# State-space outputs beside the gate projections in a fused three-block kernel

## The chip, the cores and the metric

The kernel runs on one core of a Trainium2 chip. The metric is the device time of one execution in microseconds (us). The core has TensorE (PE in the profile; its weight loads are PEld), VectorE (DVE), ScalarE (ACT), GpSimd (POOL) and SyncE (SP), which issues the DMAs. Each engine works through its own queue in order.

## The reference

Three residual blocks run one after the other on a 1024 x 1024 activation: an attention block, a gated linear attention block and a state-space (S5) block. Only the last is touched:

```python
proj = h @ w_in
u, z = jnp.split(proj, [D_INNER], axis=-1)
...
bu = lax.complex(jnp.einsum('blgi,gpi->blgp', u32, jnp.real(b_bar)),
                 jnp.einsum('blgi,gpi->blgp', u32, jnp.imag(b_bar)))
...
_, states = lax.associative_scan(combine, (a, bu), axis=1)
y = (jnp.einsum('blgp,gip->blgi', jnp.real(states), c_re.astype(f32))
     - jnp.einsum('blgp,gip->blgi', jnp.imag(states), c_im.astype(f32)))
y = y + d_skip.astype(f32) * u32
y = jax.nn.gelu(y.reshape(bsz, seqlen, D_INNER))
y = y * jax.nn.sigmoid(y @ w_glu.astype(f32) + b_glu.astype(f32))
y = y * jax.nn.silu(z.astype(f32))
return y.astype(h.dtype) @ w_out
```

There are 128 groups of 16 channels; eight groups make an octet, so there are sixteen octets of 128 channels. The sequence is cut into 128 chunks of eight steps: within a chunk everything is a matrix product, and only the state at the chunk borders is scanned.

## The kernel before, in words

All products are made in float32r with a high and a low half, three matmuls for each (`mm3`, L190: L192 high x high, L193 high x low, L194 low x high). The weight stream `WStream` (L43) loads a piece of 128 x 1024 floats, casts its high half (L177, ACT) and subtracts the low half (L185, POOL or DVE) into a ring of six slots. Pieces are split in the order of `put`; a piece may be split as soon as fewer than six pieces ahead of it are unreleased (`pump`, L112), and a piece with a gate waits for that as well.

The S5 block (`s5`, L2125) has these stages:

- First stage (loop over `first`): the sixteen projections of u, then z's first three, and three steps behind them `states(o)`: chunk border inputs into `X` (128 states x 128 chunks x 128 groups, groups innermost) and the within-chunk part of y, which goes to DRAM (`yp_d`). After each fourth octet a scan over the borders is queued; its steps are DVE instructions on `X` (L2213 to L2265), issued a few at a time by `scan_on`.
- Gate stage (loop over `second`): the thirteen other projections of z, each 48 matmuls of 512 columns and a silu on ACT (L2154), with six scan steps behind each.
- Output stage (loop over `o`): for each octet the states' product (24 matmuls of 128 columns into a PSUM tile `big`, from `X` split into halves and the matrix `v_mat`), the sum with the stored part (L2361, DVE), gelu (L2366, ACT), and two octets later `y_out`: eight transposes (L2316), a cast (L2317) of the first half and a copy (L2319) of the second, and the low half (L2320). Beside it the first product of the GLU is begun (`glu_early`).
- GLU and output projection, in two halves of 512 columns: `gate` forms y times silu(z) beside the matmuls, then the sigmoid (L2467) and the halves of q (L2469, L185).

PSUM has four banks of 512 columns (`bank`) and two double banks (`big`). A scan holds two of the four banks; the staging pool `w4` has three tiles. `v_mat`'s low halves go to POOL for octets 0 to 3 and to DVE after that.

Of the kernel before, what the change touches and what calls it, by code (L numbers as in the profile page):

```python
# [21 lines left out]
S = 1024  # L22
# [2065 lines left out]
def s5_pieces(g):  # L2088

    A, ws = g.A, g.ws  # L2090
    w_in = A["s5_w_in_2"][0]
    q = Ctx()
    q.u_d = u_d = g.dram.tile([8, 16, P, P], F, name="su_d")
    q.spilled = spilled = [False] * S5_NO
    q.octet = octet = lambda o: slice(o * 8, o * 8 + 8)

    def put_u(o):
        return ws.put(8, P, [((slice(None),) * 3, u_d.rearrange("t i g c -> (t i) g c")[:, octet(o), :])],
                      gate=lambda: spilled[o], lo="dve")
# [12 lines left out]

    def put_cols(w, nk, c0, lo=None):
        return [ws.put(8, P, [((slice(None),) * 3, g.kview(w, k0 * P, 8, c0, P))], lo=lo) for k0 in range(0, nk, 8)]

    q.put_m, q.put_cols = put_m, put_cols
    q.first = []
    for i in range(S5_NO + S5_LAG):
        px = [put_u(i - S5_LAG), put_m(g.w_mat, i - S5_LAG, "pool"), put_T(i - S5_LAG)] if i >= S5_LAG else None
        q.first.append((i, px, put_cols(w_in, 8, i * P, "dve" if i == 1 else "pool")))  # L2120
    q.second = [(i, put_cols(w_in, 8, 2048 + i * P, "pool")) for i in range(S5_LAG, S5_NO)]
    return q


def s5(g, xn3, xstack, out):  # L2125
# [1 line left out]
    w_glu = A["s5_w_glu_2"][0]  # L2127
    w_out = A["s5_w_out_2"][0]
    NO, LAG = S5_NO, S5_LAG
    EARLY, GLU_AT, GLU_N = 1, (8, 14), 2  # L2130
    q = g.pieces.pop("s5") if "s5" in g.pieces else s5_pieces(g)
    u_d, spilled, octet, put_m, put_cols, first, second = (
        q.u_d, q.spilled, q.octet, q.put_m, q.put_cols, q.first, q.second)

    z_d = g.dram.tile([NO, P, S], F, name="sz_d")
    yp_d = g.dram.tile([NO, P, S], F, name="syp_d")
# [10 lines left out]
    def project(i, ids):  # L2147

        W = ws.take(ids)
        stage = stg.tile([P, S], F, name="w4")  # L2150
        for half in range(2):
            ps = g.bank()
            gemm_tr(g, hT, half, W, 0, P, ps, ids if half else None, True, later)
            nc.scalar.activation(half_of(stage, half, True), ps.rearrange("p (t c) -> p t c", t=8),  # L2154
                                 AF.Copy if i < NO else AF.Silu)
            ws.pump(1)
            if half == 0:
                yield
# [20 lines left out]
    third, pglu, pout = [], [[[] for _ in range(EARLY)], []], []  # L2179
    for o in range(NO):  # L2180
        if o in GLU_AT:
            for e in range(EARLY):
                pglu[0][e] += put_cols(w_glu[GLU_AT.index(o) * 1024:], 8, e * P)
        third.append([put_m(g.v_mat, o, "dve" if o > 3 else "pool"),
                      ws.put(8, P, X[:, :, octet(o)].rearrange("p n g -> p g n"), gate=lambda o=o: scanned[o // 4])])
# [4 lines left out]
    def states(o, ids):  # L2190

        U, W = ws.take(ids[:2])
        ps = g.big().rearrange("p (g n) -> p g n", g=8)
        for j in range(8):
            g.mm3(ps[:, j], [a[:, j, :] for a in W], [a[:, j, :] for a in U], True, True)
        nc.scalar.copy(X[:, 1:P, octet(o)], ps.rearrange("p g n -> p n g")[:, 0:P - 1])
        del ps
        yield
        T = ws.take(ids)[2]
        yp = stg.tile([P, 8, 8, 16], F, name="w4")  # L2200
        ps = g.big().rearrange("p (g n) -> p g n", g=8)
        for j in range(8):
            g.mm3(ps[:, j], [a[:, j, :] for a in U], [a[:, j, :] for a in T], True, True)
        nc.scalar.copy(yp.rearrange("c t g o -> c g t o"), ps.rearrange("c g (t o) -> c g t o", t=8))
        del ps
        ws.release(ids)
        nc.sync.dma_start(yp_d[o], yp.rearrange("c t g o -> c (t g o)"))
        ws.pump(2)

    G4, J = 32, 16  # L2210
# [66 lines left out]
    for i, px, pp in first:  # L2277
        gens = [states(i - LAG, px)] if px else []
        gens.append(project(i, pp) if i else begun)
        for _ in range(2):  # L2280
            for ge in gens:
                next(ge, None)
                scan_on(1)
        if px and (i - LAG) % 4 == 3:
            scans.append(((i - LAG) // 4, scan((i - LAG) // 4)))
    per = 6
    ws.hi_eng, ws.lo_eng = ["act"], ["pool"]
    early = []
    for i, ids in second:
        if i == NO - 1:  # L2290
            for o in range(2):
                early.append(stg.tile([P, 8, P], F, name="w4"))
                nc.sync.dma_start(early[o], yp_d[o].rearrange("c (t x) -> c t x", t=8))
        for _ in project(NO + i, ids):
            pass
        scan_on(per)
    assert not scans
    hold.clear()
    hp.close()

# [6 lines left out]
    ypend = deque()  # L2307

    def load_yp(o):
        nc.sync.dma_start(f32(y_hl[:, o]), yp_d[o].rearrange("c (a x) -> c a x", a=2))  # L2310

    def y_out():
        o, ya = ypend.popleft()
# [9 lines left out]
    accs, glu_w, glu_k = {}, {}, [0] * EARLY  # L2323

    def glu_step(half, e, k, ps):

# [7 lines left out]
    def glu_early(last, n):
        for e in range(EARLY):
            for _ in range(n):
                k = glu_k[e]
                if k > last:
                    break
                if k == 0:  # L2340
                    accs[e] = g.bank()
                glu_step(0, e, k, accs[e])
                glu_k[e] += 1

    AHEAD = 3
    ws.hi_eng, ws.lo_eng = ["act"], ["pool"]
    for o in range(2, AHEAD):
        load_yp(o)
    ws.pump(ws.RING)
    ws.age = 1  # L2350
    for o in range(NO):
        V, X_ = ws.take(third[o])
        ya = early[o] if o < 2 else stg.tile([P, 8, P], F, name="w4")
        if len(ypend) > 1:
            y_out()
        ps = g.big()
        for j in range(8):
            g.mm3(ps[:, j * P:(j + 1) * P], [b[:, j, :] for b in X_], [b[:, j, :] for b in V], True, True)
        part = ya.rearrange("c t x -> c (t x)") if o < 2 else f32(y_hl[:, o]).rearrange("c a x -> c (a x)")
        y4, part = [a.rearrange("c (t g o) -> c t g o", t=8, g=8) for a in (ya.rearrange("c t x -> c (t x)"), part)]  # L2360
        nc.vector.tensor_tensor(y4, part, ps.rearrange("c (g t o) -> c t g o", g=8, t=8), OP.add)  # L2361
        ws.release(third[o])
        ws.pump(3)
        if o >= GLU_AT[0] + 2:
            glu_early(o - 3, GLU_N)
        nc.scalar.activation(ya, ya, AF.Gelu_apprx_tanh)  # L2366
        ypend.append((o, ya))
        if o + AHEAD < NO:
            load_yp(o + AHEAD)
    glu_early(NO - 3, NO)  # L2370
    y_out()
    y_out()
# [197 lines left out]
```

## Time and profile before

| what | us |
|---|---|
| median of 3 runs (2654.11 to 2659.1) | 2658.63 |
| the profiled execution: its own time | 2654.64 |
| its span | 2652.9 |
| busy in the span: PE / PEld / DVE / ACT / POOL | 2440.0 / 1996.0 / 1675.6 / 1130.8 / 1024.5 |
| gate stage, to its last z matmul | to 2014.2 |
| output stage | 2014.2 to 2122.2 |

Times in the trace are us from the span's start. An engine's busy time says little by itself; what matters is which engine the others wait for in a stage. PE durations in the timeline overlap (they include the pipeline), so a matmul's cost is the distance from one start to the next.

### The profile page before, as it was taken

Reading aid. Unit: us, or ns where it says so; the run is one execution under the profiler, and the core shown is the slowest. Engines: PE = TensorE matmul, PEld = TensorE weight load, DVE = VectorE, ACT = ScalarE, POOL = GpSimd, SP = SyncE. Lnnn points to the kernel's source line nnn. Section 1 sums busy time; section 2 is a strip of 40 time slices with the busy share of each in tenths; the row PEclk is TensorE's granted clock in tenths of the full one; section 3 lists DMA queues with packets and bytes.
Section 4 is the critical chain, followed back from the end, with each engine's and each line's share of the span. In section 5 each row is a group of like instructions: output and inputs, shape, how many; then the busy total and the mean of one; then the engine's idle time right before and its main releaser. Section 6 shows DMA issues by size and latency. Waiting matters only on the chain.

```text
span 2652.9 us, 33078 instructions
## 1 busy us (share of the span) xinstructions
PE 2440.0 (92%) x11817; PEld 1996.0 (75%) x11817; DVE 1675.6 (63%) x2970; ACT 1130.8 (43%) x1907; POOL 1024.5 (39%) x780
## 2 busy tenths in 40 slices
PE   5887976999999999998988899999996999999998
PEld 4665654787777777777777778888885888888887
DVE  5888676777454666785777750376998855425632
ACT  5458895556432222325434334444223832223321
POOL 3515553322201566663444414444322632332321
PEclk8998987899999999999988999999997899999999
DMA  8312124221333554545333217777433753444441
GB/s 266 105 36 70 50 84 140 84 65 54 117 115 103 141 144 144 160 153 177 119 104 109 78 61 196 199 192 202 143 98 106 248 152 118 147 139 139 147 139 56
DMA packets 330173, 338.25 MB, mean 127 GB/s; under 512 B 67366, under 2 KB 248182, under 8 KB 329752
## 3 DMA queue, kind: packets, MB, share of 16 engines
q1 hardware_dynamic: 330008, 336.13, 41.3%
q8 instruction: 93, 1.52, 0.2%
q14 instruction: 72, 0.59, 0.1%
HBM read 239.19 MB, written 96.87 MB: 127 GB/s over the span
## 4 chain that ended last, share of the span: by engine, by line
PE 63%; DVE 16%; ACT 8%; issue 7%; POOL 2%; DMA 2%; SPq 1%; DVEq 0%; ACTq 0%; POOLq 0%
PE mm L192 16%; PE mm L194 16%; PE mm L193 16%; PE big L194 3%; PE big L193 3%; PE big L192 3%; ACT tku L828 2%; PE big L1160 1%; PE mm L1675 1%; DVE whl L185 1%; DVE xacc L1988 1%; PE mm L1259 1%; DVE rs_t L213 1%; ACT tka_d L837 1%; POOL rs_h L210 1%
## 5 line engine op out<-in xcount | busy, mean ns | idle before, releaser
L185 POOL TENSOR_TENSOR whl<-wraw,whl 128x1024 fp32r<-128x1024 f32 x158 | 386.5, 2454 | 862.8 <-ACT whl L177 777.1
L177 ACT CAST whl<-wraw 128x1024 fp32r<-128x1024 f32 (+1 forms) x279 | 287.9, 1048 | 396.0 <-PE mm L194 265.2
L185 DVE TENSOR_TENSOR whl<-wraw,whl 128x1024 fp32r<-128x1024 f32 (+2 forms) x121 | 181.7, 1510 | 295.7 <-ACT whl L177 295.5
L192 PE MATMUL mm<-h_hi,whl 128*128 128x512 f32 x768 | 306.2, 399 | 3.8 <-ACT uT L966 2.3
L192 PE MATMUL mm<-whl,h_hi 128*128 128x512 f32 (+1 forms) x720 | 290.0, 403 | 16.7 <-ACT whl L177 11.6
L194 PE MATMUL mm<-h_hi,whl 128*128 128x512 f32 x768 | 302.5, 394 | 0.0
L193 PE MATMUL mm<-h_lo,whl 128*128 128x512 f32 x768 | 302.5, 394 | 0.0
L193 PE MATMUL mm<-whl,h_hi 128*128 128x512 f32 (+1 forms) x720 | 283.4, 394 | 7.7 <-DVE whl L185 7.7
L194 PE MATMUL mm<-whl,h_lo 128*128 128x512 f32 (+1 forms) x720 | 283.2, 393 | 0.0
L193 PE MATMUL mm<-y_hl,whl 128*128 128x512 f32 x512 | 202.9, 396 | 0.5 <-DVE y_hl L2320 0.5
L192 PE MATMUL mm<-y_hl,whl 128*128 128x512 f32 x512 | 203.2, 397 | 0.0
L194 PE MATMUL mm<-y_hl,whl 128*128 128x512 f32 x512 | 202.8, 396 | 0.0
L192 PEld LDWEIGHTS mm<-h_hi,whl 128*128 128x128 f32 x768 | 144.9, 189 | 41.2 <-ACT uT L966 3.5
L192 PEld LDWEIGHTS mm<-whl,h_hi 128*128 128x128 f32 x720 | 138.6, 192 | 45.2 <-ACT whl L177 12.0
L194 PEld LDWEIGHTS mm<-h_hi,whl 128*128 128x128 f32 x768 | 144.7, 188 | 33.0
L193 PEld LDWEIGHTS mm<-h_lo,whl 128*128 128x128 f32 x768 | 144.9, 189 | 31.3 <-issue 0.2
L193 PEld LDWEIGHTS mm<-whl,h_hi 128*128 128x128 f32 x720 | 138.6, 192 | 34.4 <-DVE whl L185 9.1
L194 PEld LDWEIGHTS mm<-whl,h_lo 128*128 128x128 f32 x720 | 137.7, 191 | 29.0
L185 DVE TENSOR_TENSOR w<-w 128x512 f32<-128x512 f32 x48 | 71.4, 1513 | 105.8 <-DMA w<-sz_d 61.2
L193 PEld LDWEIGHTS mm<-y_hl,whl 128*128 128x128 f32 x512 | 96.5, 188 | 23.9 <-DVE y_hl L2320 0.9
L194 PEld LDWEIGHTS mm<-y_hl,whl 128*128 128x128 f32 x512 | 96.4, 188 | 23.4
L192 PEld LDWEIGHTS mm<-y_hl,whl 128*128 128x128 f32 x512 | 96.5, 188 | 22.9
(540 smaller groups left out, 5831.2 us busy)
## 6 DMA issues: line engine op xcount, KB each, us to landing
wraw<-in_s_w_glu_dram SPq DMA_DIRECT2D x64, 512.0 KB, 4.0
wraw<-in_gla_w_in_dram SPq DMA_DIRECT2D x40, 512.0 KB, 3.7
wraw<-in_s_w_in_dram SPq DMA_DIRECT2D x32, 512.0 KB, 4.2
wraw<-in_s_w_out_dram SPq DMA_DIRECT2D x32, 512.0 KB, 3.5
gv_d<-stg SPq DMA_DIRECT2D x32, 256.0 KB, 2.2
v_mat<-vc SPq DMA_DIRECT2D x32, 256.0 KB, 2.6
w_mat<-wo SPq DMA_DIRECT2D x32, 256.0 KB, 2.4
gz_d<-stg SPq DMA_DIRECT2D x32, 256.0 KB, 2.1
```

The source lines that it names most:

```text
L177: nc.scalar.copy(out, in_)
L185: e.tensor_tensor(out, a, b, op)
L192: nc.tensor.matmul(out, lhsT=lhs[0], rhs=rhs[0], start=start, stop=False)
L193: nc.tensor.matmul(out, lhsT=lhs[0], rhs=rhs[1], start=False, stop=False)
L194: nc.tensor.matmul(out, lhsT=lhs[1], rhs=rhs[0], start=False, stop=stop)
L210: nc.gpsimd.tensor_tensor(h, v, self.mhalf[:, :n], OP.pow)
L213: nc.vector.tensor_tensor(t, h, h, OP.mult)
L828: nc.scalar.activation(aj[:, :(b + 1) * P], keys[b], AF.Sign, bias=abias[:, q:q + 1], accum_out=asum[:, q:q + 1])
L837: nc.scalar.activation(asgn[:, c], asum[:, c], AF.Sign, bias=aneed[:, c])
L1160: nc.tensor.matmul(ps[:, c0:c1], lhsT=qt[:, j, :], rhs=kT[:, h // 4, e, c0:c1], start=(e == 0), stop=(e == 1))
L1259: nc.tensor.transpose(ps[:, o:o + P], sms[e][:, jj * P:(jj + 1) * P], g.ident)
L1675: nc.tensor.matmul(ps[0:16, i * P:(i + 1) * P], lhsT=B1[:, g0 + i, :], rhs=vc[:, i, 0:8, :].rearrange("p k o -> p (k o)"), start=True, sto ...
```

## The change

Twelve of the sixteen octets' output products move into the gate stage, one behind each of the first twelve z projections there. Their sum and gelu are written back into the octet's place in `X`, over its states, and the transposes read them there. Four octets stay in the output stage, where three `y_out` stand behind each product. z is stored as it comes; silu(z) is made in `gate` as z times sigmoid(z). The stored part of y keeps the matmul's layout. The scans get two steps instead of one in the second half of each step of the first stage, and four instead of six for each z projection.

```diff
-    q.second = [(i, put_cols(w_in, 8, 2048 + i * P, "pool")) for i in range(S5_LAG, S5_NO)]
+    q.put_z = lambda i: put_cols(w_in, 8, 2048 + i * P, "pool")
...
             nc.scalar.activation(half_of(stage, half, True), ps.rearrange("p (t c) -> p t c", t=8),
-                                 AF.Copy if i < NO else AF.Silu)
+                                 AF.Copy)
...
+    def put_out(o):
+        third.append([put_m(g.v_mat, o, "pool" if o < BESIDE else "dve"),
+                      ws.put(8, P, X[:, :, octet(o)].rearrange("p n g -> p g n"), gate=lambda: scanned[o // 4])])
+    for i in range(LAG, NO):
+        second.append((i, q.put_z(i)))
+        if i - LAG < BESIDE:
+            put_out(i - LAG)
...
-        nc.scalar.copy(yp.rearrange("c t g o -> c g t o"), ps.rearrange("c g (t o) -> c g t o", t=8))
+        nc.scalar.copy(yp.rearrange("c (g x) -> c g x", g=8), ps)
...
-                scan_on(1)
+                scan_on(1 + r)
...
+    def products(o):
+        V, X_ = ws.take(third[o])
+        ps = g.big()
+        for j in range(8):
+            g.mm3(ps[:, j * P:(j + 1) * P], [b[:, j, :] for b in X_], [b[:, j, :] for b in V], True, True)
+        ws.release(third[o])
+        ws.pump(2)
+        sums.append((o, ps))
+    def outputs():
+        o, ps = sums.popleft()
+        Xo = X[:, :, octet(o)]
+        gto = lambda a: a.rearrange("p (g t o) -> p g t o", g=8, t=8)
+        nc.vector.tensor_tensor(Xo.rearrange("p (g o) t -> p g t o", g=8), gto(parts.pop(o)), gto(ps), OP.add)
+        del ps
+        yield
+        nc.scalar.activation(Xo, Xo, AF.Gelu_apprx_tanh)
-    for i, ids in second:
...
-        for _ in project(NO + i, ids):
-            pass
-        scan_on(per)
+    for n, (i, ids) in enumerate(second):
+        ge, ou = project(NO + i, ids), outputs() if sums else iter(())
+        next(ge)
+        next(ou, None)
+        scan_on(2)
...
+        if n < BESIDE:
+            load_part(n)
+            products(n)
+        scan_on(2)
...
-            nc.tensor.transpose(pb[t // 4][:, t % 4 * P:(t % 4 + 1) * P], ya[:, t], g.ident)
+            nc.tensor.transpose(pb[t // 4][:, t % 4 * P:(t % 4 + 1) * P], X[:, :, o * 8 + t], g.ident)
         nc.scalar.copy(y_hi[:, o], pb[0])
         stage = wpool.tile([P, 512], F, name="w2")
-        nc.vector.tensor_copy(stage, pb[1])
+        g.copy("act" if o % 2 else "dve", stage, pb[1])
...
+    for o in range(BESIDE, NO):
+        if o + 1 < NO:
+            load_part(o + 1)
+        products(o)
+        ou = outputs()
+        for n in range(3):
+            y_out(done)
+            done += 1
+            next(ou, None)
+            ws.pump(1)
+            glu_early(2, done - 3)
...
         g.tt("dve" if e % 2 else "pool", t[:, 0], t[:, 0], t[:, 1], OP.mult)
+        nc.scalar.activation(t[:, 1], t[:, 1], AF.Sigmoid)
+        g.tt("pool" if e % 2 else "dve", t[:, 0], t[:, 0], t[:, 1], OP.mult)
```

First place: ACT's queue in the gate stage before, two z projections (`w` is the staging tile, with two evacuations for each).

```order
L2154 ACTIVATE w_17304<-mm 128x8x64
L177 CAST whl<-X 128x1024
L2154 ACTIVATE w_17304<-mm 128x8x64
L2154 ACTIVATE w_17393<-mm 128x8x64
L177 CAST whl<-wraw 128x1024
L2154 ACTIVATE w_17393<-mm 128x8x64
```

The same queue and stage in the changed kernel, one z projection and the start of the next:

```order
L2154 ACTIVATE w_16920<-mm 128x8x64
L177 CAST whl<-wraw 128x1024
L2154 ACTIVATE w_16920<-mm 128x8x64
L2318 ACTIVATE X<-X 128x128x8
L177 CAST whl<-wraw 128x1024
L177 CAST whl<-X 128x1024
L2154 ACTIVATE w_17052<-mm 128x8x64
```

A gelu (L2318) and the casts of `v_mat` and of an octet's states moved between the evacuations of two projections.

Second place: DVE's queue before, at the end of the last scan (L2262 is a scan's last instruction).

```order
L2262 TENSOR_TENSOR X<-X,mm 128x15x32
L2361 TENSOR_TENSOR w_17681<-w_17681,big_17751 128x1024
L2361 TENSOR_TENSOR w_17683<-w_17683,big_17785 128x1024
L185 TENSOR_TENSOR whl<-wraw,whl 128x1024
L2319 COPY w_17833<-mm 128x512
```

DVE's queue in the changed kernel, at the end of the last scan (there L2269):

```order
L2269 TENSOR_TENSOR X<-X,mm 128x15x32
L2315 TENSOR_TENSOR X<-w_17972,big_17974 128x8x8x16
L185 TENSOR_TENSOR whl<-wraw,whl 128x1024
L2315 TENSOR_TENSOR X<-w_18088,big_18090 128x8x8x16
L185 TENSOR_TENSOR whl<-wraw,whl 128x1024
L179 COPY w_18238<-mm 128x512
```

Before, the sums of all octets stood behind the whole scan, from octet 0 on; in the changed kernel only those of octets 10 to 15 (L2315) do, and those of 0 to 9 stand among the scan's steps.

Third place: PE's queue before, where the output stage's first transposes stand.

```order
L194 MATMUL big_17785<-whl 128x128
L2316 MATMUL mm<-ident,w_17681 128x128 x8
L192 MATMUL big_17837<-whl 128x128
L193 MATMUL big_17837<-whl 128x128
L194 MATMUL big_17837<-whl 128x128
```

PE's queue in the changed kernel at its first transposes, behind the product of octet 12:

```order
L194 MATMUL big_18196<-whl 128x128
L2348 MATMUL mm<-ident,X 128x128 x24
L192 MATMUL mm<-y_hl,whl 128x512
L193 MATMUL mm<-y_hl,whl 128x512
L194 MATMUL mm<-y_hl,whl 128x512
L192 MATMUL big_18282<-whl 128x128
```

ACT's queue in the changed kernel at the same place (L2349 evacuates the first half of an octet of y, L177 COPY the second of every other one):

```order
L177 CAST whl<-wraw 128x1024
L177 CAST whl<-X 128x1024
L2349 CAST y_hl<-mm 128x512 x2
L177 COPY w_18256<-mm 128x512
L2318 ACTIVATE X<-X 128x128x8
L2349 CAST y_hl<-mm 128x512
L177 CAST whl<-wraw 128x1024
L177 CAST whl<-X 128x1024
```

Eight transposes behind each product became twenty-four, read from `X`, and two split casts stand ahead of the first evacuations.

## Rows read from the trace of the kernel before

**Rows 1.** Busy time by stretch: each engine's us (instructions), granted PE clock, DMA share, GB/s.

```profile
1600.00:1870.00 270.00, 270.00 (x1563) 235.34 (x1562) 129.79 (x297) 116.48 (x133) 121.58 (x51) 1.00 0.71 195
1870.00:2014.00 144.00, 144.00 (x622) 116.89 (x621) 130.94 (x348) 29.39 (x39) 35.33 (x15) 1.00 0.36 113
2019.50:2043.50 24.00, 0.32 (x3) 0.18 (x3) 22.29 (x53) 3.09 (x4) 5.09 (x2) 0.54 0.08 25
2200.00:2250.00 50.00, 50.00 (x216) 40.23 (x215) 24.43 (x19) 14.87 (x18) 15.63 (x8) 1.00 0.40 119
```

**Rows 2.** Timeline of PE: end of the z projections, waits of the output stage.

```profile
2014.20 0.22 PE L192 MATMUL big<-whl 128*128 128x128 f32 x1
...
2043.35 1.97 PE L2316 MATMUL mm<-ident,w 128*128 128x128 f32 x8 [23.68 <-ACT w L2366]
...
2072.52 1.90 PE L2316 MATMUL mm<-ident,w 128*128 128x128 f32 x8 [1.71 <-ACT w L2366]
...
2122.22 0.49 PE L193 MATMUL mm<-y_hl,whl 128*128 128x512 f32 x1 [0.45 <-DVE y_hl L2320]
```

**Rows 3.** Chain that ended last (start, us), about the end of the scan.

```profile
2039.76 0.64 DVE mm L2261
2041.00 1.23 DVE w L2361
2042.24 1.06 ACT w L2366
```

**Rows 4.** Timeline of PE, one octet of the output stage at full clock.

```profile
2095.75 0.45 PE L192 MATMUL mm<-y_hl,whl 128*128 128x512 f32 x1
...
2097.19 1.04 PE L2316 MATMUL mm<-ident,w 128*128 128x128 f32 x8
2097.99 0.31 PE L192 MATMUL big<-whl 128*128 128x128 f32 x1
...
2100.70 0.44 PE L192 MATMUL mm<-y_hl,whl 128*128 128x512 f32 x1
```

**Rows 5.** Short stretches of the output stage, columns as in rows 1.

```profile
2072.00:2077.00 5.00, 4.48 (x26) 4.49 (x27) 4.97 (x5) 4.90 (x6) 2.46 (x2) 0.66 0.95 353
...
2087.00:2092.00 5.00, 5.00 (x19) 4.32 (x19) 4.12 (x4) 3.95 (x5) 1.55 (x2) 0.50 0.94 287
```

**Rows 6.** Groups of instructions, 2014 to 2122: busy us, mean ns, idle before.

```profile
L185 POOL TENSOR_TENSOR whl<-X,whl 128x1024 fp32r<-128x1024 f32 x14 | 41.2, 2942 | 57.0 <-ACT whl L177 52.1 <-DVE w L2361 3.5 <-DVE whl L185 1.5
L177 ACT CAST whl<-X 128x1024 fp32r<-128x1024 f32 x14 | 28.5, 2036 | 5.4 <-PE big L194 4.1 <-PE mm L194 1.3
L177 ACT CAST whl<-wraw 128x1024 fp32r<-128x1024 f32 x20 | 20.9, 1055 | 5.2 <-issue 3.2 <-ACT y_hl L2317 1.0 <-DMA wraw<-in_s_w_glu_dram 0.9
L2366 ACT ACTIVATE w<-w 128x1024 f32<-128x1024 f32 x16 | 17.0, 1062 | 24.5 <-DVE w L2361 24.4
L2361 DVE TENSOR_TENSOR w<-y_hl,big 128x1024 f32<-128x1024 f32 x14 | 16.9, 1210 | 3.3 <-PE big L194 3.3
L185 POOL TENSOR_TENSOR whl<-wraw,whl 128x1024 fp32r<-128x1024 f32 x6 | 14.3, 2408 | 0.0
L2320 DVE TENSOR_TENSOR y_hl<-mm,y_hl 128x512 fp32r<-128x512 f32 x16 | 10.9, 684 | 8.2 <-ACT y_hl L2317 8.2
L2317 ACT CAST y_hl<-mm 128x512 fp32r<-128x512 f32 x16 | 9.2, 574 | 1.2 <-PE mm L2316 1.2
```

**Rows 7.** Groups of instructions, gate stage (1870 to 2014).

```profile
L2239 DVE TENSOR_TENSOR mm<-X,mm 64x256 f32<-64x256 f32 x60 | 25.8, 430 | 2.1
L2262 DVE TENSOR_TENSOR X<-X,mm 128x480 f32<-128x480 f32 x28 | 18.3, 653 | 1.0
...
L2154 ACT ACTIVATE w<-mm 128x512 f32<-128x512 f32 x26 | 15.5, 595 | 53.4 <-issue 42.3 <-DMA sz_d<-w 7.8 <-PE mm L194 3.3
```

**Rows 8.** Instructions on the staging tile: count, ns least/median/most, first and last start.

```profile
L2467 ACT ACTIVATE w<-mm,cols x32: 667/684/691, 2130.6 to 2558.2; 128x512 f32<-128x512 f32 x32
...
L185 POOL TENSOR_TENSOR w<-w x16: 1289/1528/1754, 2129.3 to 2538.4; 128x512 f32<-128x512 f32 x16
```

More of the change, by code (lines that the diff above doesn't have):

```diff
@@ L2129, in s5 @@
     NO, LAG = S5_NO, S5_LAG
-    EARLY, GLU_AT, GLU_N = 1, (8, 14), 2
+    BESIDE = 12
     q = g.pieces.pop("s5") if "s5" in g.pieces else s5_pieces(g)
-    u_d, spilled, octet, put_m, put_cols, first, second = (
-        q.u_d, q.spilled, q.octet, q.put_m, q.put_cols, q.first, q.second)
+    u_d, spilled, octet, put_m, put_cols, first = (
+        q.u_d, q.spilled, q.octet, q.put_m, q.put_cols, q.first)
     z_d = g.dram.tile([NO, P, S], F, name="sz_d")
@@ L2178, in s5 @@
     nc.gpsimd.memset(X[:, 0], 0.0)
[L2179 to L2185, printed above, removed]
+    second, third, pglu, pout = [], [], [[[]], []], []
+    def put_out(o):
[6 more added lines that the diff above has]
+    for o in range(BESIDE, NO):
+        if o % 2 == 0:
+            pglu[0][0] += put_cols(w_glu[(o - BESIDE) * 512:], 8, 0)
+        put_out(o)
     for half in range(2):
@@ L2199, in states @@
         T = ws.take(ids)[2]
-        yp = stg.tile([P, 8, 8, 16], F, name="w4")
+        yp = stg.tile([P, S], F, name="w4")
         ps = g.big().rearrange("p (g n) -> p g n", g=8)
@@ L2203, in states @@
             g.mm3(ps[:, j], [a[:, j, :] for a in U], [a[:, j, :] for a in T], True, True)
-        nc.scalar.copy(yp.rearrange("c t g o -> c g t o"), ps.rearrange("c g (t o) -> c g t o", t=8))
+        nc.scalar.copy(yp.rearrange("c (g x) -> c g x", g=8), ps)
         del ps
         ws.release(ids)
-        nc.sync.dma_start(yp_d[o], yp.rearrange("c t g o -> c (t g o)"))
+        nc.sync.dma_start(yp_d[o], yp)
         ws.pump(2)
@@ L2279, in s5, with load_part @@
         gens.append(project(i, pp) if i else begun)
-        for _ in range(2):
+        for r in range(2):
             for ge in gens:
                 next(ge, None)
-                scan_on(1)
+                scan_on(1 + r)
         if px and (i - LAG) % 4 == 3:
             scans.append(((i - LAG) // 4, scan((i - LAG) // 4)))
-    per = 6
-    ws.hi_eng, ws.lo_eng = ["act"], ["pool"]
-    early = []
-    for i, ids in second:
[L2290 to L2293, printed above, removed]
-        for _ in project(NO + i, ids):
-            pass
-        scan_on(per)
-    assert not scans
+    parts, sums = {}, deque()
+    def load_part(o):
+        parts[o] = stg.tile([P, S], F, name="w4")
+        nc.sync.dma_start(parts[o], yp_d[o])
+    def products(o):
[14 more added lines that the diff above has]
+        nc.scalar.activation(Xo, Xo, AF.Gelu_apprx_tanh)
+    ws.hi_eng, ws.lo_eng = ["act"], ["pool"]
+    for n, (i, ids) in enumerate(second):
[3 more added lines that the diff above has]
+        scan_on(2)
+        for _ in ge:
+            pass
+        for _ in ou:
+            pass
+        if n < BESIDE:
+            load_part(n)
+            products(n)
+        scan_on(2)
+    assert not scans and not sums
     hold.clear()
@@ L2306, in s5, with y_out @@
     wpool = pool_of(g, xp, "s5w", bufs=2)
[L2307 to L2313, printed above, removed]
+    def y_out(o):
         pb = [g.bank(), g.bank()]
         for t in range(8):
-            nc.tensor.transpose(pb[t // 4][:, t % 4 * P:(t % 4 + 1) * P], ya[:, t], g.ident)
+            nc.tensor.transpose(pb[t // 4][:, t % 4 * P:(t % 4 + 1) * P], X[:, :, o * 8 + t], g.ident)
         nc.scalar.copy(y_hi[:, o], pb[0])
         stage = wpool.tile([P, 512], F, name="w2")
-        nc.vector.tensor_copy(stage, pb[1])
+        g.copy("act" if o % 2 else "dve", stage, pb[1])
         nc.vector.tensor_tensor(y_lo[:, o], pb[0], f32(y_hi[:, o]), OP.subtract)
         nc.sync.dma_start(y_d[o], stage)
-    accs, glu_w, glu_k = {}, {}, [0] * EARLY
+    accs, glu_w = {}, {}
+    glu_k = [0]
     def glu_step(half, e, k, ps):
@@ L2332, in glu_step, with glu_early @@
             ws.release(ids)
[L2334 to L2348, printed above, removed]
+    def glu_early(n, last):
+        while n and glu_k[0] <= last:
+            if glu_k[0] == 0:
+                accs[0] = g.bank()
+            glu_step(0, 0, glu_k[0], accs[0])
+            glu_k[0] += 1
+            n -= 1
     ws.pump(ws.RING)
     ws.age = 1
[L2351 to L2372, printed above, removed]
+    load_part(BESIDE)
+    done = 0
+    for o in range(BESIDE, NO):
+        if o + 1 < NO:
[8 more added lines that the diff above has]
+            glu_early(2, done - 3)
+    while done < NO:
+        y_out(done)
+        done += 1
+        ws.pump(1)
+        glu_early(2, done - 3)
     xp.close()
@@ L2453, in s5 @@
         for e in range(NO):
-            k0 = glu_k[e] if half == 0 and e < EARLY else 0
+            k0 = glu_k[0] if half == 0 and e == 0 else 0
             ps = accs.pop(e) if k0 else g.bank()
```

## The prediction

> **What bounds the kernel now.** I read the table of slices first, to find where TensorE is not busy late in the span, then busy times by stretch, then the timeline of TensorE there, then the chain. TensorE is busy without a break, at full clock, through the first S5 stage and the gate stage [rows 1], and again in the GLU. Between lies the output stage: 108.0 us from the first product behind the z matmuls, 2014.2, to the end of the last wait for an octet of y, 2122.2 [rows 2]. In 2019.5 to 2043.5 TensorE works 0.32 of 24 us while DVE works 22.29 [rows 1]: two products are through, and then transposes wait 23.68 us for gelu [rows 2], which waits for a sum that stands on DVE behind the last scan's steps [rows 3]. So here the scan ends last, not TensorE.
>
> What TensorE would need for the stage at full clock comes from one undisturbed octet [rows 4]: two GLU steps 2095.75 to 2097.19, 1.44 us (0.72 each); eight transposes to 2097.99, 0.80 us (0.10 each); 24 product matmuls to 2100.70, 2.71 us. Sixteen products 43.4, 128 transposes 12.8, fourteen GLU steps 10.1: 66.3 us. The other 41.7 of 108.0 are lost: 23.7 in the one wait, some 4 in short ones, the rest, 14, to the clock, which is at 0.50 to 0.66 in stretches after waits of a microsecond or two [rows 2, 5]. No change to this stage alone can bring more than 41.7 us.
>
> **The change, part by part.**
> Products into the gate stage. Twelve products of 2.71 us go behind z projections: 32.5 us. TensorE is without a break there, so nothing hides them; the gate stage ends at 2014.2 + 32.5 = 2046.7 if its feeders keep up. Per z projection TensorE then takes 11.1 (144 us for 13 [rows 1]) + 2.7 = 13.8 us. ACT's part: three split casts, two of 1.06 and one of 2.04, gelu 1.06 [rows 6], two evacuations of 0.60 [rows 7]: 6.4. POOL's: two low halves of 2.41 and one of 2.94 [rows 6]: 7.8. DVE's: four scan steps and a sum. Most steps are five instructions of some 0.43, 2.3 us with their gaps; in a scan's last stretch, seven steps, a step has two of 0.65 [rows 7], two nearly as long and five small ones, 3.6 us. That is 9 to 14.5 us a projection and 1.2 for the sum, over 13.8 only in a last stretch. All fit, and the ring lets a piece be split two octets ahead, 27 us. I take 0 for waits; from nothing to 1 us for each of twelve octets, 12 us, stays in the range. Below 0 it can't go, since TensorE had no gap there.
>
> More scan steps in the first stage. DVE works 129.8 of 270 us there [rows 1]; six steps instead of four for each 16.5 us (a projection of 11.1 and two states products of 2.7) make six times 2.3, 13.9 us, and 1.2 for u's low half. It still fits, and the low half of u, which shares DVE, is split more than one projection ahead. 0, and up to 3 if one end of a scan (3.6 us a step) delays it. What it buys: with six steps in each of the twelve rounds that have a scan, 72 instead of 48 are through before the gate stage, so 44 of 116 (29 for each scan) remain, 11 projections' worth at four. The scan is done before 2046.7, and the wait of 23.7 us has nothing left to wait for.
>
> The output stage that remains. TensorE: four products 10.8, 128 transposes 12.8, fourteen GLU steps 10.1: 33.7 us. What is late next is the evacuation. y_out needs two of three or four banks, and a bank comes free by ACT's cast (0.57) and DVE's low half (0.68), or by the copy of the same size [rows 6]. After each of the first two products ACT has a `v_mat` and an X split ahead of the casts, 1.06 + 2.04 = 3.1 us, which start only when the product has released its slots. First round: casts until +3.2, cast of y +3.8, low half +4.6, so the third octet's transposes start 3 us late; the next bank waits behind a sum of 1.21 on DVE: another 1.1. Second round, the same with one bank less: 3.1. Third and fourth round, two casts of w_glu in place of the X split: 1.2 each. The last four octets: DVE and ACT need 2.25 where TensorE needs 1.52: 2.9 in all. Together 12.5 us. From half of that, if TensorE's lead hides more, to 20.
>
> The transposes read X. Their data was one block; now each element lies 512 bytes behind the one before. No transpose of the trace does that. The nearest rows are the splits: ACT's cast takes 2036 ns from X against 1055 from a loaded piece, a factor of 1.93; POOL's 2942 against 2408, 1.22 [rows 6]. Bounds: nothing (0.10 each) up to ACT's 1.99 ns an element, 0.255 for 128, +19.8 us for 128 transposes. I take ACT's factor, 0.193: +11.9, of which the six octets of the two rounds that wait for ACT hide theirs: 7.4 us. DVE's write into X has the same stride and may double 1.21; it is off the path but for the one place above.
> [...]
>
> The clock. After waits of one or two microseconds it fell to 0.50 to 0.66 for some five us at a time while TensorE was 90% busy or more [rows 2, 5]. The first two rounds have such waits, but there ACT ends last, not TensorE. I take 2 us; from 0 to 10.
>
> silu taken apart. One more sigmoid on ACT, about the GLU's own 0.68, and one more product on DVE or POOL, at most POOL's 1.53 [rows 8], for each of 32 tiles. In the GLU ACT works 14.9, POOL 15.6 and DVE 24.4 of 50 us [rows 1], 11.1 us of TensorE's work for each tile, and nothing on TensorE waits for q before the output projection. 0; 2 us at most, for a late split.
>
> Sum: the output stage takes 33.7 + 12.5 + 7.4 + 2 = 55.6 and ends at 2046.7 + 55.6 = 2102.3, against 2122.2: 19.9 us less. Behind it all is as before. From the profiled execution's 2654.64 that makes 2634.7; the median of the runs is 4.0 above that execution, and from it I get 2638.7. I say 2637.
>
> **The rivals.**
> (a) No price on reading X and none by the clock: the stage takes 46.2, the gain is 29.3, the time 2625 to 2629. For it: a transpose's 0.10 us may have room for slower reads, and POOL lost only a factor of 1.22 [rows 6].
> [...]
> [...]
> (c) The gate stage isn't fed: TensorE waits for the X splits on ACT and POOL, 1 us an octet. That is +12, and the gain 8: 2647 to 2651. Against it: casts stand two octets ahead, and ACT and POOL have half of their time free.
> (d) Slower: the transposes from X take much longer than the splits show. The place is the weight load, 128 on TensorE's path in the output stage. The stage may take 2122.2 - 2046.7 = 75.5 us before nothing is gained; without transposes it has 10.8 + 10.1 + 12.5 + 2 = 35.4, so the point is 40.1 / 128 = 0.313 us a transpose, three times 0.10. At four times, 0.40, the stage is 86.6 and the kernel 11 us slower: 2666 to 2670. Against it: ACT's own rate would make 0.255.
>
> **How the numbers follow.** The forecast, 2631 to 2645, has 0.47; (a) 0.25; (b), or the upper bound of the X read with a slow clock, 0.11; (c) 0.09; (d) 0.08. A measurement of this kernel can tell about 0.2%, 5.3 us. Faster by more than that: the forecast, (a), (c) and a little of (b), 0.82. Same: most of (b), 0.10. Slower: (d), 0.08. The range runs from (a) with half of the evacuation's waits, a gain of 35 to 37 and so 2621, to (b) without gain, 2655; (d) and the tail beyond (a) are left out.
>
> **What would show it.** Right: TensorE without a gap and at clock 1.00 until about 2047; no wait over 5 us behind it; DVE's last scan step before 2030; the GLU's first full product at about 2102 instead of 2122. The transposes' distance of start to start tells (a), the forecast and (d) apart: 0.10, 0.19, over 0.31. Gaps ahead of L2348 released by ACT's cast or DVE's low half in the first two rounds show the evacuation. Wrong: waits of TensorE on L177 or L185 between z projections (c), a clock near 0.5 through the output stage (b), or a GLU that takes longer than before.

## The result and the profile after

The changed kernel takes 2673.2 us (median of four runs), the kernel before 2657.8 beside it: a ratio of 1.0062 (95% interval 1.0044 to 1.0079), 0.6% slower where 0.8% faster was forecast. One more run, the one profiled first, had a granted clock of 0.65 throughout, took 3524.9 us and is not used. The profile below is of an execution of 2671.92 us (span 2670.2), taken beside one of 2657.13 of the kernel before; lines of the kernel before are from the profile of span 2652.9. Ahead of this profile I had expected the loss in the output stage, with transposes 0.35 us or more apart and the z matmuls ending near 2047. Neither came; a third guess, a longer GLU, did.

Profiled executions differ by up to 8 us ahead of the S5 block, so I count from its first evacuation (L2154, first start in the row): 1578.0 before, 1578.5 after. Landmarks of the changed kernel, PE by line: last z matmul, first transposes, first full GLU step behind the last transposes, first matmul of the output projection. The instructions by tile, with first and last start:

```profile
L2154 ACT ACTIVATE w<-mm x64: 586/597/656, 1578.5 to 2062.0; 128x512 f32<-128x512 f32 x64
L194 PE MATMUL mm<-h_hi,whl x207: 390/393/404, 1880.2 to 2059.0; 128*128 128x512 f32 x104
L192 PE MATMUL big<-whl,q_hi x18: 388/389/395, 2287.4 to 2309.8; 128*128 128x512 f32 x18
```

The timeline of PE, start and duration:

```profile
2061.94 2.58 PE L2348 MATMUL mm<-ident,X 128*128 128x128 f32 x16
...
2117.89 0.48 PE L192 MATMUL mm<-y_hl,whl 128*128 128x512 f32 x1
```

The first and the last of the tile rows in the kernel before:

```profile
L2154 ACT ACTIVATE w<-mm x64: 582/597/602, 1578.0 to 2016.4; 128x512 f32<-128x512 f32 x64
L192 PE MATMUL big<-whl,q_hi x16: 388/390/393, 2290.8 to 2309.2; 128*128 128x512 f32 x16
```

The loss against the forecast falls into three pieces, counted in spans. The z matmuls end at 2059.0, 480.5 from the landmark, where 2046.7 was forecast (468.7): +11.8. The output stage takes 58.9 where 55.6 was forecast: +3.3. From the output projection's first matmul to the span's end it is 382.8, against 362.1 before: +20.7, where nothing was forecast. Together 35.8 of the 37.2 by which the span misses the forecast's 2633.0 (2652.9 less 19.9); the rest is 0.5 at the landmark and 0.9 in the first half of the GLU.

Busy time by stretch, columns as in rows 1, after:

```profile
1600.00:1850.00 250.00, 250.00 (x1451) 217.70 (x1450) 155.03 (x353) 104.01 (x120) 105.95 (x45) 1.00 0.72 189
1850.00:1870.00 20.00, 14.25 (x60) 11.18 (x59) 12.14 (x29) 6.05 (x7) 10.26 (x5) 0.74 0.55 170
1870.00:2050.00 180.00, 180.00 (x938) 152.52 (x938) 158.31 (x334) 75.18 (x74) 89.62 (x35) 1.00 0.50 157
2200.00:2250.00 50.00, 50.00 (x217) 40.54 (x216) 29.30 (x24) 17.45 (x23) 16.41 (x10) 1.00 0.36 106
2420.00:2470.00 50.00, 44.47 (x184) 35.46 (x183) 23.93 (x30) 15.23 (x25) 13.39 (x9) 0.93 0.46 137
```

The wait of 23.7 us of [rows 2] is gone and from 1870 to 2050 the gate stage runs without a gap, as forecast; then a matmul of its last z projection waits 2.76 us. But 5.75 us of TensorE's time are lost at the end of the first stage, with the clock at 0.74 there. And the GLU, which looks untroubled in the stretch that answers to the last of [rows 1], loses 5.5 us in 2420 to 2470. Waits of PE after, in time: in the first stage, in the last z projection for a bank that the scan uses (L2268 is a scan step), and in the GLU (timeline, idle time and releaser in brackets):

```profile
1855.13 0.33 PE L193 MATMUL big<-whl 128*128 128x128 f32 x1 [1.62 <-DVE whl L185]
1860.83 0.80 PE L192 MATMUL mm<-h_hi,whl 128*128 128x512 f32 x1 [2.92 <-ACT whl L177]
1863.26 0.80 PE L194 MATMUL mm<-h_hi,whl 128*128 128x512 f32 x1 [1.21 <-POOL whl L185]
2053.54 0.50 PE L192 MATMUL mm<-h_hi,whl 128*128 128x512 f32 x1 [2.76 <-DVE mm L2268]
2458.53 0.79 PE L192 MATMUL mm<-y_hl,whl 128*128 128x512 f32 x1 [5.53 <-ACT w L2492]
2572.14 0.79 PE L192 MATMUL mm<-whl,q_hi 128*128 128x512 f32 x1 [7.16 <-ACT w L2492]
2576.59 0.80 PE L192 MATMUL mm<-whl,q_hi 128*128 128x512 f32 x1 [2.80 <-ACT w L2492]
```

L2492 is the GLU's sigmoid, which empties the accumulator (L2467 before). What stands ahead of it, on ACT, and on SP (SPq: time in SP's queue, waiting included), after:

```profile
2457.28 0.63 ACT L2425 ACTIVATE w<-w 128x512 f32<-128x512 f32 x1 [12.99 <-DVE w L185]
...
2560.99 0.63 ACT L2425 ACTIVATE w<-w 128x512 f32<-128x512 f32 x1 [5.90 <-POOL w L185]
2561.53 0.67 ACT L2492 ACTIVATE w<-mm,cols 128x512 f32<-128x512 f32 x1
...
2563.51 1.99 ACT L177 CAST whl<-wraw 128x1024 fp32r<-128x1024 f32 x2
2570.88 0.63 ACT L2425 ACTIVATE w<-w 128x512 f32<-128x512 f32 x1 [5.38 <-DVE w L185]
```

```profile
2555.81 0.43 SPq L2419 DMA_DIRECT2D w<-sz_d  x1
2557.70 8.48 SPq L100 DMA_DIRECT2D wraw<-in_s_w_out_dram  x2
2566.22 0.43 SPq L2419 DMA_DIRECT2D w<-sz_d  x1
2568.05 8.57 SPq L100 DMA_DIRECT2D wraw<-in_s_w_out_dram  x2
```

This is a closed loop. The new sigmoid L2425, of the next tile, waits for z's product; that waits for z's load (L2419); SP issues this only when its two loads of weights have found raw slots (the stream's three tiles for loaded pieces that are not yet split), after 8.5 us; the slots come free by ACT's casts (L177) and the low halves made from them, and the casts stand behind L2425. So the GLU's own sigmoid, whose matmuls are done, waits some 5.5 us in every tile, and longer where stores of finished rows stand in SP's queue too (12.99 us ahead of 2457.28); there TensorE runs out of banks.

The slots' part of the loop isn't new. Waits of DVE's products and of ACT's cast of q in the GLU before (us in total, times, longest):

```profile
DVE w L185 <- DMA w<-sz_d: 61.2, 16, 7.0
ACT q_hi L2469 <- DVE w L185: 127.8, 31, 13.8
```

There too products waited for z's load, the cast of q stood behind them, and casts of weights behind that: in the longest of these waits SP's two loads found slots only after 8.54 us (from 2444.85); away from stores it took 4.2 to 4.7 us there, and 8.5 after. What did not stand behind those waits is the sigmoid that empties the accumulator (it waited for z's load once, 6.7 us), and TensorE has no wait behind 2125 in that trace.

### The profile page after: what moved, and what is told of

Its sections match the earlier page's. It is cut to its first block, busy times and chain, and to the rows that moved or that the text cites. A ratio compares the mean times of both kernels' runs of the same rounds, so it can differ in the third digit from the quotient of the medians.

```text
span 3523.1 us, 33099 instructions
## 1 busy us (share of the span) xinstructions
PE 3459.2 (98%) x11817; PEld 2308.1 (66%) x11817; DVE 1608.5 (46%) x2970; ACT 1157.9 (33%) x1946; POOL 1051.0 (30%) x804
## 4 chain that ended last, share of the span: by engine, by line
PE 93%; issue 2%; DVE 2%; ACT 1%; POOL 1%; DMA 0%; SPq 0%; DVEq 0%; POOLq 0%; ACTq 0%
PE mm L192 24%; PE mm L194 24%; PE mm L193 24%; PE big L194 4%; PE big L193 4%; PE big L192 4%; PE big L1160 2%; PE mm L1259 1%; PE mm L1675 1%; PE big L720 1%; PE mm L1227 1%; PE mm L1682 1%; PE mm L1225 1%; PE mm L1968 1%; PE mm L949 0%
## 5 line engine op out<-in xcount | busy, mean ns | idle before, releaser
L185 POOL TENSOR_TENSOR whl<-wraw,whl 128x1024 fp32r<-128x1024 f32 x167 | 412.6, 2477 | 1340.1 <-ACT whl L177 1079.8
L177 ACT CAST whl<-wraw 128x1024 fp32r<-128x1024 f32 (+1 forms) x279 | 286.8, 1046 | 560.2 <-PE mm L194 487.9
L192 PE MATMUL mm<-h_hi,whl 128*128 128x512 f32 x768 | 408.6, 532 | 0.0
L193 PE MATMUL mm<-h_lo,whl 128*128 128x512 f32 x768 | 403.9, 526 | 0.0
L194 PE MATMUL mm<-h_hi,whl 128*128 128x512 f32 x768 | 403.5, 525 | 0.0
L192 PE MATMUL mm<-whl,h_hi 128*128 128x512 f32 (+1 forms) x720 | 380.2, 528 | 0.0
L193 PE MATMUL mm<-whl,h_hi 128*128 128x512 f32 (+1 forms) x720 | 376.3, 523 | 0.8 <-DVE whl L185 0.8
L194 PE MATMUL mm<-whl,h_lo 128*128 128x512 f32 (+1 forms) x720 | 373.9, 519 | 0.0
L185 DVE TENSOR_TENSOR whl<-wraw,whl 128x1024 fp32r<-128x1024 f32 (+2 forms) x112 | 153.2, 1375 | 448.4 <-ACT whl L177 448.4
L192 PE MATMUL mm<-y_hl,whl 128*128 128x512 f32 x512 | 261.6, 511 | 0.0
L194 PE MATMUL mm<-y_hl,whl 128*128 128x512 f32 x512 | 260.1, 508 | 0.0
L193 PE MATMUL mm<-y_hl,whl 128*128 128x512 f32 x512 | 259.8, 507 | 0.0
L192 PEld LDWEIGHTS mm<-h_hi,whl 128*128 128x128 f32 x768 | 170.3, 222 | 94.9 <-issue 35.5
L194 PEld LDWEIGHTS mm<-h_hi,whl 128*128 128x128 f32 x768 | 167.2, 218 | 92.3 <-issue 34.9
L194 PEld LDWEIGHTS mm<-whl,h_lo 128*128 128x128 f32 x720 | 154.2, 214 | 87.4 <-issue 33.7
L193 PEld LDWEIGHTS mm<-whl,h_hi 128*128 128x128 f32 x720 | 153.0, 213 | 83.4 <-issue 34.7
L192 PEld LDWEIGHTS mm<-whl,h_hi 128*128 128x128 f32 x720 | 151.1, 210 | 83.5 <-issue 34.1
L194 PEld LDWEIGHTS mm<-y_hl,whl 128*128 128x128 f32 x512 | 106.1, 207 | 60.7 <-issue 20.0
L193 PEld LDWEIGHTS mm<-y_hl,whl 128*128 128x128 f32 x512 | 106.5, 208 | 59.2 <-issue 20.0
L192 PEld LDWEIGHTS mm<-y_hl,whl 128*128 128x128 f32 x512 | 106.3, 208 | 59.3 <-issue 20.1
```

The source lines that it names most:

```text
L177: nc.scalar.copy(out, in_)
L185: e.tensor_tensor(out, a, b, op)
L192: nc.tensor.matmul(out, lhsT=lhs[0], rhs=rhs[0], start=start, stop=False)
L193: nc.tensor.matmul(out, lhsT=lhs[0], rhs=rhs[1], start=False, stop=False)
L194: nc.tensor.matmul(out, lhsT=lhs[1], rhs=rhs[0], start=False, stop=stop)
```

## The experiments

Ten kernels, beside the execution above; each ratio is against the kernel before on the same chip. Kernels that ran on different chips are compared by these ratios, times 2657 us.

**The silu alone.** In the kernel before:

```diff
-AF.Copy if i < NO else AF.Silu)
+AF.Copy)
...
+        nc.scalar.activation(t[:, 1], t[:, 1], AF.Sigmoid)
+        g.tt("pool" if e % 2 else "dve", t[:, 0], t[:, 0], t[:, 1], OP.mult)
```

> The kernel before with one part of the change alone: gate's silu taken apart (projection copied, a sigmoid on ACT and a second product in the gated linear unit). Theory: the whole loss after 2119 us comes from this part, because the new sigmoid stands in ACT's queue ahead of the sigmoid that empties the accumulator of the tile before, and ahead of the casts that free the raw slots for which SP's queue waits before it issues the load of z: the stretch from the output projection's begin to the end, and the gated linear unit ahead of it, take 14 to 22 us more than in the kernel before, so about 2672 to 2680. Rival: the loss came from another part (the order of the products and of the loads, late output octets), and the sigmoid costs nothing, as the prediction had it: 2655 to 2660, and no wait of PE for w of the gated linear unit over 3 us.

Measured: 2685.3, ratio 1.0101 (1.0084 to 1.0118), 28 us slower; PE's waits for the GLU's sigmoid (L2469 here) 17.9 us in 4, and 387.3 us from the output projection's first matmul to the end, against 362.1. Above the theory's range, and far from the rival: this part alone turns the kernel before into a slower one.

**The silu undone** (the same lines of the changed kernel, the other way).

> The changed kernel with this one part undone: the gate projections are evacuated through Silu again, and the gated linear unit has one product per tile. Theory: the waits of 5.5, 7.2 and 2.8 us of PE for the sigmoid of the gated linear unit go, and the clock with them: 15 to 21 us less than the changed kernel, 2651 to 2658. On the other side stand two changes of ACT's function table per gate tile (Silu and Gelu in turns) in the gate stage, where ACT is under half busy: 0 to 5 us. Rival: the waits belong to the loads and stay: 2670 to 2676.

Measured: 2651.5, ratio 0.9977 (0.9967 to 0.9986), some 23 us less than the changed kernel. No wait of PE behind 2130 is left, and the rest from the output projection's first matmul takes 362.1 us again.

**The silu apart, but later in the queue.**

```diff
             g.sub("dve", q_lo[:, e], t[:, 0], f32(q_hi[:, e]))
+            if e + 1 < NO:
+                gate2(e + 1, zs[0])
```

`gate2` holds the sigmoid and the second product, taken out of `gate`.

> The changed kernel with silu still apart, but the new sigmoid and product of tile e+1 are written behind the sigmoid, product, cast and difference of tile e. Theory (the place in ACT's queue is what costs): the accumulator of tile e is emptied whatever the load of z does, the three waits go, 12 to 21 us less than the changed kernel: 2651 to 2660. Rival (the extra work on ACT, DVE and POOL is what costs, or the raw slots wait for the sigmoid all the same): 2666 to 2676.

Measured: 2651.9, ratio 0.998 (0.997 to 0.999), some 22 us less, with the same work as the changed kernel. The line of the stretch in which the changed kernel lost 5.5 us:

```profile
2420.00:2470.00 50.00, 50.00 (x216) 40.24 (x215) 28.94 (x38) 17.58 (x28) 17.14 (x12) 1.00 0.46 135
```

The rest takes 362.2 us. So the place in the in-order queue costs all of it, and the extra work nothing. ACT and SP in this kernel:

```profile
2460.56 0.63 ACT L2427 ACTIVATE w<-w 128x512 f32<-128x512 f32 x1 [1.99 <-POOL w L185]
2461.10 1.99 ACT L177 CAST whl<-wraw 128x1024 fp32r<-128x1024 f32 x2
...
2445.65 9.25 SPq L100 DMA_DIRECT2D wraw<-in_s_w_glu_dram  x2
```

The casts that free the slots still stand behind the new sigmoid (L2427 here), and SP still waits for slots, without cost to TensorE. What counts is that the sigmoid that empties the accumulator no longer stands behind the new one.

**u's low halves on POOL** in the first stage of the changed kernel.

```diff
-                      gate=lambda: spilled[o], lo="dve")
+                      gate=lambda: spilled[o], lo="pool")
```

> The changed kernel with one edit in the first stage: the low halves of u are made on POOL instead of DVE, so that no raw slot waits behind the doubled scan steps of DVE. Theory: PE's idle 5.7 us near 1855 to 1866 and the low clock behind them go, 8 to 12 us less than the changed kernel: 2660 to 2666. Rival 1: the first loads of the scan's tables stay late behind the raw loads, and the idle time moves to the gate stage: 2668 to 2676. Rival 2: POOL, which then has 12 differences of about 1.5 us per 50 us instead of 9, holds the slots instead: 2672 or more.

Measured: 2663.5, ratio 1.0024 (1.0012 to 1.0037), some 10 us less. The stretch that had 14.25 us at clock 0.74:

```profile
1850.00:1870.00 20.00, 20.00 (x119) 17.54 (x119) 16.65 (x40) 8.86 (x10) 9.51 (x4) 1.00 0.66 201
```

What had happened there, on DVE, SP and ACT of the changed kernel:

```profile
1853.29 0.65 DVE L2269 TENSOR_TENSOR X<-X,mm 128x480 f32<-128x480 f32 x1
1853.86 1.22 DVE L185 TENSOR_TENSOR whl<-wraw,whl 128x1024 fp32r<-128x1024 f32 x1
1862.08 0.23 DVE L2238 COPY mm<-scL 128x64 f32<-128x64 f32 x1 [7.00 <-DMA scL<-scan_d]
```

```profile
1841.20 6.25 SPq L100 DMA_DIRECT2D wraw<-kp_d  x8
1855.10 0.40 SPq L100 DMA_DIRECT2D wraw<-in_s_w_in_dram  x1
...
1856.17 0.54 SPq L2227 DMA_DIRECT2D scL<-scan_d  x1
```

```profile
1844.07 1.06 ACT L177 CAST whl<-wraw 128x1024 fp32r<-128x1024 f32 x1 [7.24 <-DMA wraw<-su_d]
...
1859.73 1.04 ACT L177 CAST whl<-wraw 128x1024 fp32r<-128x1024 f32 x1 [8.21 <-DMA wraw<-in_s_w_in_dram]
```

u's cast (its piece is loaded from su_d) was done at 1845.13, but its low half stood behind scan steps on DVE until 1855.08. Only then was its raw slot free, and SP issued the next load at 1855.10, the first since 1847.45; ACT's next cast waited 8.21 us for it, and PE behind that. From the S5 landmark to the last matmul of the projection ahead of the first product it is 292.0 us in the changed kernel (1870.54 less 1578.5) and 282.7 here (1865.04 less 1582.3): 9.3 us. To the last z matmul it is 480.5 and 473.0: the wait for the scan's bank is still there (2.7 us), and behind it matmuls of 512 columns lie 0.43 us apart from 2049.92 to 2052.90 here, while they lay 0.23 apart behind it in the changed kernel (2053.88 to 2058.99).

**Both edits.**

> Both edits in the changed kernel: the new sigmoid and product of tile e+1 behind those of tile e, and the low halves of u on POOL. Theory: the two causes are separate (one ends at 1870, the other begins after 2119), so their gains add: 22 us and 11 us less than the changed kernel, 2639 to 2646. Rival: one is hidden behind the other, or both are the clock's doing: 2649 to 2656.

Measured: 2643.5, ratio 0.9951 (0.9938 to 0.9965), some 29 us less than the changed kernel where the two gains make 32: within the noise the gains add, and the kernel is faster than before.

**The stored part loaded before the gate tile** instead of behind it, on top of both.

```diff
+        if n < BESIDE:
+            load_part(n)
         next(ge)
...
-            load_part(n)
             products(n)
```

> The kernel with both edits, and one more in the gate stage: the part of an octet is loaded before the gate tile whose products need it instead of behind it, so that DVE's sums no longer wait for it (18.7 us in 7 waits in the stretch after 1860 with u on POOL). Theory (the sums' waits push the last scan steps from about 2030 to 2049, and ACT's cast of octet 12 waits for these): the last product of octet 12 ends up to 9 us earlier, 4 to 9 us less than with both edits alone. Rival (DVE's own work in the gate stage sets the scan's end): within 2 us of it. A buffer of the same pool is held longer, which can cost on the other side: up to 3 us more.

Measured: 2635.3, ratio 0.9921 (0.9908 to 0.9935), 8 us less than with both: within the theory. DVE's last scan step, with both edits and with the third:

```profile
2048.57 0.65 DVE L2269 TENSOR_TENSOR X<-X,mm 128x480 f32<-128x480 f32 x1
```

```profile
2038.21 0.65 DVE L2269 TENSOR_TENSOR X<-X,mm 128x480 f32<-128x480 f32 x1
```

The z matmuls of this kernel, with their first and last start:

```profile
L194 PE MATMUL mm<-h_hi,whl x200: 390/392/404, 1880.2 to 2051.4; 128*128 128x512 f32 x100
```

The wait for the scan's bank is gone with it: 468.5 us from the landmark to the last z matmul, 473.0 with both edits. This is the fastest version measured, with the last one below.

**The sum in another order**, on top of both edits: `p g o t` in place of `p g t o` on either side, so that writes go in runs of 32 bytes and reads are strided.

> The kernel with both edits, and the sum walked in another order: the same elements, written in runs of 32 bytes and read with a stride from PSUM and from the part, instead of written with a stride of 512 bytes (1.99 us each). Theory (the stride of the writes sets the doubled duration): 1.2 to 1.4 us each, 16 sums, DVE 10 us freer in the gate stage and the end of the scan earlier by as much of it as lies in DVE's queue: 2 to 6 us less. Rival (the strided reads cost what the strided write did): 1.9 to 2.4 us each, within 2 us.

Measured: 2645.3, ratio 0.9963 (0.995 to 0.9975), no gain. The sums, in this kernel and in the one with both edits (least/median/most ns):

```profile
L2315 DVE TENSOR_TENSOR X<-w,big x16: 1890/1950/2153, 1898.2 to 2096.9; 128x1024 f32<-128x1024 f32 x16
```

```profile
L2315 DVE TENSOR_TENSOR X<-w,big x16: 1869/1992/2335, 1895.6 to 2097.2; 128x1024 f32<-128x1024 f32 x16
```

The durations are the rival's: with strided reads the sum takes as long as with strided writes. Whether it is the reads, or the writes in short runs, isn't separated.

**Transposing a matrix whose columns lie side by side**, on top of both edits.

```diff
-X[:, :, o * 8 + t], g.ident)
+g.ident if o < BESIDE else X[:, :, o * 8 + t], g.ident)
```

> The kernel with both edits, with the source of 96 of the 128 transpositions replaced by the identity matrix, whose columns lie side by side (octets 0 to 11 of the output stage are left out of the result). Theory (the stride of 512 bytes between the columns of X slows the weight load): about 0.10 us each instead of 0.16, and since PE waits for the evacuations between them, 0 to 6 us less. Rival 1 (evacuation bounds the stage): the transpositions get shorter and the time stays within 1 us. Rival 2 (stride costs nothing, 0.16 is the clock): duration and time as before.

Measured: 2640.1, ratio 0.9943 (0.9931 to 0.9956), 3.4 us less than with both; the two intervals overlap, so the time alone doesn't settle it. Weight loads of the transposes from the identity and from X (ns) in this kernel, and then the timeline of eight transposes with the instruction behind them, first of this kernel, then of the one with both edits:

```profile
L2348 PEld LDWEIGHTS mm<-ident x96: 137/141/231, 2058.0 to 2097.3; 128*128 128x128 f32 x96
L2348 PEld LDWEIGHTS mm<-ident,X x32: 222/256/266, 2098.0 to 2106.4; 128*128 128x128 f32 x32
```

```profile
2083.34 1.04 PE L2348 MATMUL mm<-ident 128*128 128x128 f32 x8
2084.13 0.48 PE L192 MATMUL mm<-y_hl,whl 128*128 128x512 f32 x1
```

```profile
2087.48 1.30 PE L2348 MATMUL mm<-ident,X 128*128 128x128 f32 x8
2088.55 0.48 PE L192 MATMUL mm<-y_hl,whl 128*128 128x512 f32 x1
```

From start to start eight take 1.07 us from X and 0.79 from the identity, 0.134 against 0.099 each. My 0.16 in the expectation was the timeline's duration of eight, 1.30 us, divided by eight; the instruction behind them starts after 1.07. 96 times 0.035 is 3.4 us. So the stride costs 0.035 us a transposition from start to start, which rules out the second rival. Whether all of it reaches the kernel's time isn't shown: the output stage took 51.4 us here and 57.1 with both edits, but the same stage took 53.8 with u's low halves alone.

**The scan's pace undone**: one step at a time in the first stage as before, six for each gate tile, on top of the late sigmoid.

> The changed kernel with the late sigmoid (2651.9), and the scan's pace of the first stage put back to that of the kernel before, one step at a time; each gate tile then makes 6 steps instead of 4. Theory (the doubled steps of the first stage hold u's low half, a raw slot and SP's queue): PE's idle time and low clock at 1850 to 1870 go, as with the low halves on POOL. But the 24 steps move into the gate stage, where DVE is busy 26 to 28 of 30 us, so the scan, and with it octet 12, ends later than with the low halves on POOL: 2643 to 2656, and the last scan step behind 2050. Rival (the first stage lost its time for another reason, the tables' load or the order of the raw loads): PE idle as before at 1850 to 1870, 2652 to 2662.

Measured: 2679.6, ratio 1.008 (1.0066 to 1.0094), some 27 us more than with the late sigmoid alone; both expectations missed. The end of the first stage was as the theory had it, but DVE was then the bound of the gate stage, and the last z matmul came 514.6 us behind the landmark. Stretches, and PE's waits from 1840 to 2160 (us in total, times, longest):

```profile
1850.00:1870.00 20.00, 20.00 (x113) 17.23 (x112) 8.07 (x19) 10.60 (x11) 11.06 (x5) 1.00 0.65 199
...
1990.00:2020.00 30.00, 23.15 (x101) 19.82 (x102) 28.11 (x62) 11.75 (x12) 14.63 (x6) 0.73 0.27 80
```

```profile
PE mm L192 <- DVE mm L2268: 20.3, 1, 20.3
PE big L192 <- DVE X L2315: 12.3, 1, 12.3
```

The doubled pace was needed; what had to be moved out of its way was u's low half.

**Three edits, with silu as before**: is taking it apart worth anything in the right place?

> The kernel with all three edits (late sigmoid, u's low halves on POOL, part loaded a tile earlier: 2635), but with silu as in the kernel before instead of the sigmoid apart. It asks what taking silu apart is worth once the sigmoid stands in the right place. Theory (nothing: the 20 to 26 function table loads of 1.28 us that come back lie in ACT's idle time of the gate stage): within 2 us of it, 2633 to 2638. Rival (the table loads delay the evacuation of the gate tiles or ACT's casts of X): 3 to 8 us more, and waits of PE for ACT in the gate stage.

Measured: 2635.6, ratio 0.9911 (0.9897 to 0.9924), the same as with the sigmoid apart and late. TensorE is busy 30.00 of 30 us in each stretch from 1870 to 2050 in it, so the function table loads that come back on ACT, 1.28 us each, hold up nothing.

## Why the prediction was wrong

What held: the output stage of the kernel before was bounded by the scan's end, the twelve products cost TensorE 31.6 us in the gate stage (a product takes 2.63, from 1926.86 to 1929.49, in the kernel with three edits) and run there without a gap to 2050, and the wait of 23.7 us went. With three edits the z matmuls end at 2051.4, 468.5 from the landmark at 1582.9, against 468.7 forecast; the output stage takes 52.2 (to 2103.57) against 55.6; and the rest takes 362.1, exactly as before. That version's 2635.3 (span 2635.2) is near what the sum said the changed kernel would take (span 2633.0). In part that is luck: its landmark lies 4.9 us later, which hides the 3.4 that its output stage is shorter. What the sum had wrong above all is what the other edits of the change do to queues.

1. "silu taken apart ... 0; 2 us at most" failed, and is the largest piece: 20.7 us in the trace, 22 to 23 by the runs with it undone or moved, 28 with it alone. The step argued from busy shares (ACT 14.9 of 50 us). The queue decides instead: an instruction that waits for a late load holds everything behind it, and here that was the sigmoid that empties the accumulator's bank, for which TensorE waited 15.5 us in 3. The load was late because slots came free late, and casts behind the same wait made that worse (8.5 us for SP's two loads); but with the bank emptied first TensorE waited for none of it. The prediction looked for what waits for q, not for what is queued behind the added wait.
2. "More scan steps in the first stage ... 0, and up to 3" failed: 9.3 us at the end of the stage in the trace, some 10 by the run. DVE's time was enough, as worked out (155.0 of 250 us); but u's low half, behind a row of steps, held a raw slot, and through it SP's queue. Low TensorE clock after the waits (0.50 in 1860 to 1865) is part of the price.
3. "DVE's last scan step before 2030" failed: 2053.5 (2048.3 with u on POOL). The sums wait for their parts, 11.1 us in 5 waits in front of the scan steps on DVE, and take 1.99 us instead of 1.21. The price was 2.8 us of wait for the scan's bank, and 8 us by the run that loads the parts earlier. Even there the last step came at 2038.2: DVE is busy 22 to 28 of each 30 us from 1870 to 2050, so its own work is part of it.
4. The read of X by the transposes was taken at 0.193 us and is 0.134: 4.4 us for 128 instead of 11.9, of which the sum kept 7.4. Rival (d), slower by these reads, was not what made the kernel slower. Evacuation waits of PE in the output stage are there as described (5.8, 3.7 and 3.2 us for L179, y_hl and L177, with 12.5 forecast). The clock's term, 2 us, was too small: of the stage's 58.9 us, 33.7 of work, 12.7 of waits and 4.4 for the reads leave 8.1, and the granted clock is 0.83 in 2050 to 2080 and 0.89 in 2080 to 2110 (matmuls of 512 columns lie 0.43 us apart at 2070.50 and at 2080.87, 0.23 at 2084.49). So the stage's near hit comes in part from errors that cancel. Between traces with the same code in this stage it varies from 53.8 to 58.9, so what of its 3.3 us the late scan costs isn't shown. The range's upper end, 2655, took a clock near 0.5 through the whole output stage; no run shows that term, and 0.83 and 0.89 are what the changed kernel had in its place.

None of the rivals named a wait in a queue ahead of what empties a bank or frees a slot; the slower side was put on the price of reading X only. The prediction's own signs did point there: a GLU that takes longer than before was among those of being wrong.

## What to carry over

Before an instruction with a new wait is put into an in-order queue, list what stands behind it, and ask whether the engine that matters waits for any of that (here the emptying of a bank) and whether what it waits for depends on it in turn; busy shares say nothing of either. A raw slot is held until its last reader is done (u's for 9.95 us behind its cast), so a low half that shares an engine with a long chain sets the pace of the load queue. Where a change loses, undo it part by part: here one line's place and one engine's name turned a loss of 0.6% into a gain of 0.5%, and one load issued earlier made it 0.8%.

## What the runs showed of the hardware

A stride of 512 bytes cost ACT, DVE and TensorE another factor each: in the changed kernel ACT's cast from X took 2071 ns against 1047 from a loaded piece, and DVE's sum 1.99 us against 1.21 before; TensorE's weight load took 254 ns from X (with both edits) against 141 from the identity, and a transposition 0.134 against 0.099 us from start to start. ACT's gelu on X in place, in runs of 32 bytes, takes 1057 ns, as much as the side-by-side form of [rows 6]; DVE's sum with such runs on the write side and reads 64 bytes apart still takes 1.95 us. The function table loads that come back with silu take 1.28 us each on ACT; with three edits 12 stand ahead of silu's evacuations, and they and those ahead of gelu (10 in 1870 to 2050 with silu alone undone) cost nothing that could be told (2635.6 against 2635.3 us).
